# A PEER layer on one NeuronCore: the gate matrix from packed fp32 one-hots with one matmul per token, and the fetched token block picked first

## The chip, the cores and the metric

The kernel runs on one core of a Trainium2 chip. The metric is device time in microseconds for one execution. TensorE does the matmuls, VectorE (DVE), ScalarE (ACT) and GpSimd (POOL) do the element work, and SyncE (SP) starts most of the DMAs. Each engine works through its own queue of instructions in order.

## What is computed

A diffusion layer: a token mixer (two bidirectional scans), then PEER, a product-key retrieval over 128 x 128 experts for 512 latent tokens of width 1024. The change lies in PEER:

```python
PEER_HEADS = 8; PEER_NKEYS = 128; PEER_TOPK = 16; PEER_BLOCK = 128
def block(t):                                   # 128 tokens
    q = (t @ w_query).reshape(PEER_BLOCK, PEER_HEADS, 2, PEER_DQ // 2)
    s1 = jnp.einsum('thd,nd->thn', q[:, :, 0], k1)
    s2 = jnp.einsum('thd,nd->thn', q[:, :, 1], k2)
    v1, i1 = lax.top_k(s1, PEER_TOPK)
    v2, i2 = lax.top_k(s2, PEER_TOPK)
    cand_s = (v1[..., :, None] + v2[..., None, :]).reshape(PEER_BLOCK, PEER_HEADS, PEER_TOPK * PEER_TOPK)
    cand_i = (i1[..., :, None] * PEER_NKEYS + i2[..., None, :]).reshape(...)
    top_s, pos = lax.top_k(cand_s, PEER_TOPK)
    idx = jnp.take_along_axis(cand_i, pos, axis=-1)
    g = jax.nn.softmax(top_s, axis=-1)
    act = jax.nn.gelu(jnp.einsum('thkd,td->thk', expert_u[idx], t))
    return jnp.einsum('thk,thkd->td', g * act, expert_v[idx])
```

So every token picks 8 x 16 = 128 experts, each by a pair of key numbers (k1, k2) with a weight g.

## The kernel before

Token blocks 0 to 2 (384 tokens) are computed densely: every expert is evaluated for them, 128 experts (one first key) at a time, and a gate matrix, zero for experts that a token did not pick, weights the results. Block 3's 128 tokens are computed sparsely: the picked rows are fetched by index. Behind the mixer, PEER has four stages.

*Top stage* (from about 611 us). For each of 8 heads TensorE makes queries (pq, three fp32r matmuls for one product) and scores (pss, L727, plain fp32). VectorE's `pick_head` (L893) then finds a head's best 16 of each key list and of their sums. Before the change this loop picks blocks 0 to 2; block 3's scores are set aside in S3.

*Gate stage* (from 746.66 us, first L976, to 1155.89 us, last L990). `picks` (L920) turns places into key numbers, `gate_matrix` (L950) builds, for each token, the 128 x 128 matrix G[k2, k1] = sum over the 128 picks of onehot(k2) x g onehot(k1). For that, g is split into three bf16 parts. For 8 tokens at a time VectorE writes bf16 one-hots of both keys (`oh`, L976) and multiplies the first key's by the parts (`ohg`, L980 and L983; some by ScalarE, L979); TensorE does three bf16 matmuls per token (pG, L988), ScalarE copies four tokens' result to `stage` (L989), and a DMA writes 32 tokens to DRAM (Gd, L990). Block 3's pick_heads, its picks and the list of rows to fetch (`ix`) come after block 2, in the same stage.

The *hidden* part (L1004) of a group of 128 experts belongs to no stage alone: a row block ur of the first expert matrix is loaded, split into high (uh, ScalarE) and low parts (ul, GpSimd, L1001), 24 matmuls pH (L159 to L161) follow, and a gelu writes `gel`. AHEAD = 32 of 128 hiddens are written ahead of the main part, in a ring of AHEAD + 1 gel buffers; two PSUM buffers let TensorE run further ahead.

*Main part* (L1157 on). For each group: the next hidden, rows of the second matrix (vr, split to vh and vl), the gate weights of the group read back (G, L1020, one read per four groups), gel times G (`gated`, L1014, L1023), and 18 matmuls y (`combine`). Between them 264 `fetch_jobs` (L1042) are dealt evenly: an indirect DMA on GpSimd's queue (erow, L1052, six buffers), a dot product on VectorE (L1057), for the second matrix a weighted add (L1069). A *tail* finishes.

A tile framework's scheduler orders TensorE, VectorE, ScalarE and SyncE by its own costs; GpSimd's queue follows the program's order while fetches are under way (`manual_schedule`).

Of the kernel before, what the change touches and what calls it, by code (L numbers as in the profile page):

```python
# [15 lines left out]
OP = mybir.AluOpType  # L16
# [24 lines left out]
class Net:  # L41
# [3 lines left out]
    # ---------------------------------------------------------------- constants  # L45
# [16 lines left out]
    def scan_consts(self, c, tmp):  # L62
# [20 lines left out]
        # forget-gate lower bounds, channel on partition: [128, direction, head]  # L83
# [19 lines left out]
        # per-head norm gains along the row, gate weights  # L103
# [22 lines left out]
    def norm_stats(self, pool, x, tag):  # L126
        """mean and 1/std of the rows of x [128, 1024]"""
# [15 lines left out]
    def affine(self, out, x, stats, scale, shift, shared=None):  # L143
        """(x - mean) / std * scale + shift, on VectorE or, with a pool for the scratch, on ScalarE and GpSimd"""
# [50 lines left out]
    def mods_second(self, pers, pool):  # L195
        """g1, shift2, scale2, g2 of the latent stream: rows of w_ada^T times silu(c), one column each"""
# [26 lines left out]
    def mod_row(self, pool, ps, i, name, ptag):  # L223
        """vector i of m2 as a row on every partition"""
# [40 lines left out]
    # -------------------------------------------------------- input projection  # L265
# [967 lines left out]
```

## Time and profile before

| | us |
|---|---|
| time, median of 3 runs (2144.97, 2152.53, 2152.64) | 2152.53 |
| span of the profiled execution | 2142.0 |
| time of the profiled execution, taken as the median | 2152.5 |
| TensorE busy | 2016.0 (94%) |
| VectorE busy | 1578.8 (74%) |
| ScalarE busy | 808.4 (38%) |
| GpSimd busy | 1019.9 (48%) |
| TensorE's granted clock, mean | 0.904 |

The span runs from the first to the last instruction; the 10.5 us between it and the time are what lies around it. A busy TensorE is one that has a matmul under way; whether it is at its full speed tells the granted clock (1.00 is 2.4 GHz, the lower level is 1.2 GHz). A stretch is bound by the engine that never idles in it, or by the one that the others wait for. In the tables of stretches each engine's busy microseconds stand beside the length, and the counts of instructions in brackets.

### The profile page before, as it was taken

The page shows a single profiled execution, that of the slowest core. Times are in us where ns is not written, and L with a number is a line of the kernel's source. Part 1 is how long each engine was busy: PE and PEld are TensorE (multiplying, and loading weights), DVE is VectorE, ACT ScalarE, POOL GpSimd, SP SyncE. Part 2 cuts the span into 40 slices and gives each one's busy share as a digit, 9 for nine tenths or more (in the row PEclk, how much of TensorE's full clock was granted, in tenths as well). Part 3 has the DMA queues.
Part 4 walks back from the last instruction along what each step waited for, and adds up shares of the span by engine and source line. Part 5 has one row for each costly group of instructions (what it writes and reads, how often), then busy time and mean ns, then how long its engine had stood idle before and what let it go on. Part 6 is the DMA issues. An engine that isn't in the chain of part 4 may idle for free.

```text
span 2142.0 us, 27264 instructions
## 1 busy us (share of the span) xinstructions
PE 2016.0 (94%) x9973; PEld 1692.4 (79%) x9973; DVE 1578.8 (74%) x2640; ACT 808.4 (38%) x1253; POOL 1019.9 (48%) x637
## 2 busy tenths in 40 slices
PE   7877898897999899999999999999999999999997
PEld 2766777776778767777778889999889898998886
DVE  7799764767899953444437789899888889888546
ACT  3444443444343333433344333333333333333431
POOL 2445544545553310101102477777777777787001
PEclk9988999997999966667667999999999999999998
DMA  7544111001332121221214799898998989898343
GB/s 262 173 140 136 45 40 37 33 6 55 111 128 79 48 74 71 95 107 69 108 59 161 244 330 351 298 363 307 333 331 319 332 309 345 314 337 312 128 147 140
DMA packets 153031, 389.74 MB, mean 182 GB/s; under 512 B 12672, under 2 KB 62656, under 8 KB 151360
## 3 DMA queue, kind: packets, MB, share of 16 engines
q1 hardware_dynamic: 115456, 251.66, 33.6%
q0 software_dynamic: 36864, 134.23, 17.4%
q8 instruction: 78, 1.28, 0.2%
q10 hardware_dynamic: 576, 2.10, 0.2%
q14 instruction: 57, 0.47, 0.1%
HBM read 358.59 MB, written 29.36 MB: 181 GB/s over the span
## 4 chain that ended last, share of the span: by engine, by line
PE 63%; DVE 7%; issue 4%; DMA 4%; POOL 2%; ACT 1%; POOLq 0%; SPq 0%; DVEq 0%; ACTq 0%
PE pG L988 12%; PE pH L161 7%; PE pH L159 7%; PE pH L160 7%; PE y L160 7%; PE y L161 7%; PE y L159 6%; DMA erow<-in_v_dram,ix 2%; PE pq L160 1%; PE pq L161 1%; PE pq L159 1%; DMA ur<-in_uT_dram 1%; PE psc L512 1%; POOL ul L1001 1%; PE pss L727 1%
## 5 line engine op out<-in xcount | busy, mean ns | idle before, releaser
L1001 POOL TENSOR_TENSOR ul<-ur,uh 128x1024 fp32r<-128x1024 f32 x128 | 343.8, 2686 | 538.3 <-ACT uh L999 510.2
L161 PE MATMUL pH<-hh,ul 128*128 128x384 f32 x1024 | 371.5, 363 | 4.3 <-POOL ul L1001 4.2
L159 PE MATMUL pH<-hh,uh 128*128 128x384 f32 x1024 | 370.8, 362 | 2.4 <-ACT gel L1011 2.4
L160 PE MATMUL pH<-hl,uh 128*128 128x384 f32 x1024 | 369.6, 361 | 0.0
L160 PE MATMUL y<-vl,ah 128*128 128x512 f32 x768 | 302.6, 395 | 8.1 <-DVE vl L1001 4.0
L161 PE MATMUL y<-vh,al 128*128 128x512 f32 x768 | 301.4, 393 | 0.0
L159 PE MATMUL y<-vh,ah 128*128 128x512 f32 x768 | 299.3, 391 | 1.0 <-ACT vh L999 1.0
L988 PE MATMUL pG<-ohg,oh 128*128 128x128 bf16 x1152 | 273.5, 409 | 4.6 <-DVE ohg L980 4.0
L988 PEld LDWEIGHTS <-oh 128*128 128x128 bf16 x1152 | 166.0, 148 | 102.0 <-issue 15.2
L1069 DVE SCALAR_TENSOR_TENSOR yg<-erow,act,yg 128x1024 f32<-128x1024 f32 x127 | 195.4, 1539 | 54.4 <-DMA erow<-in_v_dram,ix 52.2
L999 ACT ACTIVATE uh<-ur 128x1024 fp32r<-128x1024 f32 x128 | 135.6, 1059 | 220.3 <-PE pH L160 117.1
L159 PEld LDWEIGHTS pH<-hh,uh 128*128 128x128 f32 x1024 | 211.1, 206 | 7.8 <-ACT gel L1011 2.7
L161 PEld LDWEIGHTS pH<-hh,ul 128*128 128x128 f32 x1024 | 210.7, 206 | 6.8 <-POOL ul L1001 5.2
L160 PEld LDWEIGHTS pH<-hl,uh 128*128 128x128 f32 x1024 | 210.5, 206 | 4.9
L976 DVE TENSOR_TENSOR oh<-iotaw,kT 128x2048 bf16<-128x2048 bf16 x48 | 59.1, 1232 | 208.0 <-PE pG L988 187.5
L1057 DVE SCALAR_TENSOR_TENSOR scr<-erow,h 128x1024 bf16<-128x1024 f32 x128 | 171.9, 1343 | 32.9 <-DMA erow<-in_u_dram,ix 31.5
L1052 POOL DMA_INDIRECT erow<-in_u_dram,ix x128 | 173.7, 1357 | 32.3 <-issue 23.9
L1052 POOL DMA_INDIRECT erow<-in_v_dram,ix x128 | 168.6, 1317 | 32.7 <-issue 20.2
L160 PEld LDWEIGHTS y<-vl,ah 128*128 128x128 f32 x768 | 144.8, 188 | 41.1 <-DVE vl L1001 7.3
L1001 DVE TENSOR_TENSOR vl<-vr,vh 128x1024 fp32r<-128x1024 f32 x127 | 165.5, 1305 | 12.9 <-ACT vh L999 12.9
L999 ACT ACTIVATE vh<-vr 128x1024 fp32r<-128x1024 f32 x128 | 134.6, 1054 | 93.6 <-DMA vr<-in_v_dram 68.0
L161 PEld LDWEIGHTS y<-vh,al 128*128 128x128 f32 x768 | 144.9, 189 | 29.9
(371 smaller groups left out, 3798.6 us busy)
## 6 DMA issues: line engine op xcount, KB each, us to landing
ur<-in_uT_dram SPq DMA_DIRECT2D x128, 512.0 KB
vr<-in_v_dram SPq DMA_DIRECT2D x128, 512.0 KB
Gd<-stage SPq DMA_DIRECT2D x12, 2048.0 KB
G<-Gd SPq DMA_DIRECT2D x32, 768.0 KB
wada<-in_w_ada_dram SPq DMA_DIRECT2D x64, 256.0 KB
wraw<-in_w_cf_dram SPq DMA_DIRECT2D x24, 512.0 KB
wada<-in_w_ada_dram SPq DMA_DIRECT2D x16, 512.0 KB
wqr<-in_w_q_dram SPq DMA_DIRECT2D x14, 512.0 KB
```

What stands on the lines that cost most here:

```text
L159: mm(out, lh, rh, start=start, stop=False)
L160: mm(out, lh, rl, start=False, stop=False)
L161: mm(out, ll, rh, start=False, stop=stop)
L512: nc.tensor.matmul(p[:, c, :], E[hp[h], 1, sl], E[hp[h], 0, sl], start=True, stop=True)
L727: nc.tensor.matmul(p[:, b, :], qT[s][:, b * 128:(b + 1) * 128], self.sk[:, s, :], start=True, stop=True)
L976: nc.vector.tensor_tensor(o, self.iota16w[:, :, None].to_broadcast([128, 128, 2, B]), wide(kT[:, None, :, t0:t0 + B]), op=OP.is_equal)
L988: nc.tensor.matmul(p[:, t, :], o[:, :, 1, t4 + t], f[:, :, j, t4 + t], start=j == 0, stop=j == 2)
L999: nc.scalar.activation(hi, raw, AF.Copy)
L1001: eng.tensor_tensor(lo, raw, hi, op=OP.subtract)
L1052: nc.gpsimd.indirect_dma_start(out=e, out_offset=None, in_=a[src], in_offset=bass.IndirectOffsetOnAxis(ap=self.ix[:, j:j + 1], axis=0))
L1057: nc.vector.scalar_tensor_tensor(scr, row("u", j), 1.0, h2, op0=OP.mult, op1=OP.mult, accum_out=dots[:, j:j + 1])
L1069: nc.vector.scalar_tensor_tensor(y, row("v", j), act[:, j:j + 1], y, op0=OP.mult, op1=OP.add)
```

## The change

The gate matrix. The key numbers and g of a block are transposed onto partitions as fp32 (`kg`), with no split. Per token VectorE makes two 128 x 128 fp32 operations on the row 0, 1, 2, ...: is_equal with k2, and is_equal with k1 times g; TensorE does one fp32 matmul, and ScalarE copies four tokens as before. The one-hots have three buffers of four tokens. The write of Gd per 32 tokens stays.

The order. The top loop picks all four blocks; block 3's picks, softmax and `ix` follow at once, ahead of the gate matrix. The fetch buffers open there, and `tick` deals the 264 fetch jobs over gate matrix (0.22 units per group of four tokens, one per hidden) and main part (one per hidden, one per group). In program order 43 jobs come to lie in the gate stage. GpSimd's program order begins ahead of the gate matrix. AHEAD goes from 32 to 25, and the hiddens are written between groups of tokens, not behind each block.

```diff
-    AHEAD = 32
-    GC, OB = 2, 2
+    AHEAD = 25
+    GB, OB = 4, 3
...
-    def gate_matrix(self, w, ps, b, key, g):
+    def picks_on_partitions(self, w, ps, key, g):
         p = ps.tile([128, 4, 128], F32, name="pkT", tag="ss", bufs=2)
         for i, t in enumerate((key[:, 0], key[:, 1], g)):
-            nc.tensor.transpose(p[:, i, :], t.rearrange("p h k -> p (h k)"), self.n.ident)
...
-        for q in range(128 // self.GT):
-            stage = w.tile([128, 128, self.GT], F32, name="stage", bufs=2)
-            for t8 in range(0, self.GT, B):
...
-                nc.vector.tensor_tensor(o, self.iota16w[:, :, None].to_broadcast([128, 128, 2, B]), wide(kT[:, None, :, t0:t0 + B]), op=OP.is_equal)
...
-                        for j in range(3):
-                            nc.tensor.matmul(p[:, t, :], o[:, :, 1, t4 + t], f[:, :, j, t4 + t], start=j == 0, stop=j == 2)
...
+            self.nc.tensor.transpose(p[:, i, :], t.rearrange("p h k -> p (h k)"), self.n.ident)
+        kg = w.tile([128, 3, 128], F32, name="kg", bufs=2)
+        self.nc.scalar.activation(kg, p[:, 0:3, :], AF.Copy)
+        return kg
+    def gate_group(self, w, ps, kg, t0, out, i):
+        nc, iota = self.nc, self.n.iota_row
+        GB = self.GB
+        o = w.tile([128, GB, 2, 128], F32, name="oh12", bufs=self.OB)
+        p = ps.tile([128, GB, 128], F32, name="pG", tag=("bd", "qp")[i % 2], bufs=2)
+        for t in range(GB):
+            k1, k2, g = (kg[:, j, t0 + t:t0 + t + 1] for j in range(3))
+            nc.vector.tensor_scalar(o[:, t, 0], iota, k2, None, op0=OP.is_equal)
+            nc.vector.tensor_scalar(o[:, t, 1], iota, k1, g, op0=OP.is_equal, op1=OP.mult)
+            nc.tensor.matmul(p[:, t, :], o[:, t, 0], o[:, t, 1], start=True, stop=True)
+        nc.scalar.activation(out, p.rearrange("p t n -> p n t"), AF.Copy)
...
-                        for b in range(ND):
+                        for b in range(4):
                             self.pick_head(w, S[:, b], b, h)
+                key = self.picks(w, 3)
+                self.softmax(w, self.g[:, None])
...
+                manual.enter_context(tc.manual_schedule(engines={mybir.EngineType.Pool}))
+                jobs = self.fetch_jobs(fp, fp, yg)
+                groups = ND * 128 // self.GB
+                gcost = 0.055 * self.GB
+                total = groups * gcost + 128 + 128 - self.TAIL - 24
+                done, spent = 0, 0.0
+                def tick(u):
+                    nonlocal done, spent
+                    spent += u
+                    want = min(len(jobs), int(len(jobs) * max(0, spent - 6) / (total - 6)))
+                    for f, *args in jobs[done:want]:
+                        f(*args)
+                    done = want
...
-                        self.gate_matrix(bp, ps, b, key, g)
-                        for _ in range(self.AHEAD // ND):
-                            self.hidden(nh, up, gl, hps)
-                            nh += 1
...
+                        for _ in self.gate_block(bp, ps, b, kg):
+                            at += 1
+                            tick(gcost)
+                            while nh < self.AHEAD * at // groups:
+                                self.hidden(nh, up, gl, hps)
+                                nh += 1
+                                tick(1)
```

What stands in the engines' queues. The names end in buffer numbers; lines of the changed kernel differ: its one-hots are L967 and L968, its pG L969, its ul L992, its fetch L1043, dots L1048, adds L1058 and L1060.

VectorE in the gate stage, before (`oh12` and `ohg` for eight tokens; `oh` rows belong to the next block's picks):

```order
L980 TENSOR_TENSOR ohg_6218<-oh12_6217,gp3_6172 128x128x16
L983 TENSOR_TENSOR ohg_6218<-oh12_6217,gp3_6172 128x128x6
L976 TENSOR_TENSOR oh12_6252<-iotaw_5039,kT_6170 128x2048
L945 TENSOR_TENSOR oh_7094<-oh_7094 128x8x64
L980 TENSOR_TENSOR ohg_6253<-oh12_6252,gp3_6172 128x128x16
L983 TENSOR_TENSOR ohg_6253<-oh12_6252,gp3_6172 128x128x6
L976 TENSOR_TENSOR oh12_6287<-iotaw_5039,kT_6170 128x2048
L945 TENSOR_TENSOR oh_7094<-oh_7094 128x8x32
L980 TENSOR_TENSOR ohg_6288<-oh12_6287,gp3_6172 128x128x16
```

VectorE where block 0 ends and block 1 begins, after (`pr`, `oh`, `key`: picks; `yg`: the fetched block's sums):

```order
L945 TENSOR_TENSOR oh_7167<-oh_7167 128x8x128
L1054 TENSOR_TENSOR act_6319<-act_6319,gp_4551 128x16
L928 TENSOR_SCALAR pr_7982<-pos2_5036 128x128
L945 TENSOR_TENSOR oh_7167<-oh_7167 128x8x64
L1058 TENSOR_SCALAR yg_4901<-erow_7563,act_6319 128x1024
L945 TENSOR_TENSOR oh_7167<-oh_7167 128x8x32
L1060 SCALAR_TENSOR_TENSOR yg_4901<-erow_7646,act_6319,yg_4901 128x1024
L946 TENSOR_TENSOR key_7159<-oh_7167 128x128
L1060 SCALAR_TENSOR_TENSOR yg_4901<-erow_7664,act_6319,yg_4901 128x1024
L967 TENSOR_SCALAR oh12_7181<-iota_row_59,kg_7178 128x128
L968 TENSOR_SCALAR oh12_7181<-iota_row_59,kg_7178 128x128
```

Three wide operations per eight tokens became two small ones per token, and additions of fetched rows, the last three of a run that begins with the tenth dot, now stand ahead of block 1's first one-hot.

GpSimd where the fetches begin, before, in the main part:

```order
L1001 TENSOR_TENSOR ul_9574<-ur_9571,uh_9573 128x1024
L1001 TENSOR_TENSOR ul_9636<-ur_9633,uh_9635 128x1024
L1052 DMA erow_9695<-in_u_dram,ix_4552 128x1024
L1052 DMA erow_9698<-in_u_dram,ix_4552 128x1024
L1001 TENSOR_TENSOR ul_9704<-ur_9701,uh_9703 128x1024
L1052 DMA erow_9763<-in_u_dram,ix_4552 128x1024
L1052 DMA erow_9766<-in_u_dram,ix_4552 128x1024
L1052 DMA erow_9769<-in_u_dram,ix_4552 128x1024
```

GpSimd within the gate stage, after (erow_7480 is the sixteenth fetch, the first for which all six buffers wait for dots that stand behind block 0's one-hots):

```order
L1043 DMA erow_7462<-in_u_dram,ix_4552 128x1024
L1043 DMA erow_7480<-in_u_dram,ix_4552 128x1024
L992 TENSOR_TENSOR ul_7531<-ur_7528,uh_7530 128x1024
L1043 DMA erow_7563<-in_v_dram,ix_4552 128x1024
L992 TENSOR_TENSOR ul_7616<-ur_7613,uh_7615 128x1024
L1043 DMA erow_7646<-in_v_dram,ix_4552 128x1024
L1043 DMA erow_7664<-in_v_dram,ix_4552 128x1024
L992 TENSOR_TENSOR ul_7715<-ur_7712,uh_7714 128x1024
L1043 DMA erow_7745<-in_v_dram,ix_4552 128x1024
L1043 DMA erow_7763<-in_v_dram,ix_4552 128x1024
```

The fetches moved from the main part to the gate stage, pairwise between the ul rows that the hiddens there need.

TensorE at the end of the gate stage, before (26 of 32 hiddens are done there):

```order
L988 LDWEIGHTS oh12_8597
L988 MATMUL pG_8618<-ohg_8598,oh12_8597 128x128
L160 MATMUL pH_8804<-hl_4550,uh_8800 128x384
L161 MATMUL pH_8804<-hh_4549,ul_8801 128x384
L159 MATMUL pH_8837<-hh_4549,uh_8833 128x384
L160 MATMUL pH_8837<-hl_4550,uh_8833 128x384
```

TensorE at the end of the gate stage, after (14 pH rows follow the last pG, then the first y of the main part):

```order
L161 MATMUL pH_9015<-hh_4549,ul_9012 128x384
L969 MATMUL pG_8802<-oh12_8801 128x128
L159 MATMUL pH_9015<-hh_4549,uh_9011 128x384
L969 MATMUL pG_8802<-oh12_8801 128x128
L160 MATMUL pH_9015<-hl_4550,uh_9011 128x384
L161 MATMUL pH_9015<-hh_4549,ul_9012 128x384
L159 MATMUL pH_9015<-hh_4549,uh_9011 128x384
```

Loads of bf16 weights and three matmuls per token became one fp32 matmul per token among pH rows; in the stage there are 384 pG and 469 pH in place of 1152 and 446, with 189 pH ahead of it in place of 176, and 27 of the hiddens done at its end, where before more were left to come.

## Rows read from the trace of the kernel before

**Rows 1.** The page: the chain that ended last, by engine and line
```profile
PE pG L988 12%; PE pH L161 7%; PE pH L159 7%; PE pH L160 7%; PE y L160 7%; PE y L161 7%; PE y L159 6%; DMA erow<-in_v_dram,ix 2%; PE pq L160 1%; PE pq L161 1%; PE pq L159 1%; DMA ur<-in_uT_dram 1%; PE psc L512 1%; POOL ul L1001 1%; PE pss L727 1%
```

**Rows 2.** Stretches: start:end, length, busy us of each engine, granted clock, DMA share, GB/s
```profile
640.00:660.00 20.00, 20.00 (x104) 16.65 (x103) 18.39 (x129) 7.34 (x14) 8.34 (x4) 1.00 0.24 80
900.00:950.00 50.00, 50.00 (x200) 38.24 (x199) 21.21 (x24) 20.22 (x30) 7.65 (x3) 0.67 0.20 74
1150.00:1200.00 50.00, 45.83 (x238) 42.62 (x237) 43.74 (x117) 20.35 (x28) 25.75 (x8) 0.91 0.62 214
1300.00:1350.00 50.00, 50.00 (x255) 45.49 (x254) 48.15 (x45) 18.22 (x25) 38.79 (x25) 1.00 0.95 346
```

**Rows 3.** Timeline (start, us, engine, line), VectorE and SyncE: the gate stage's ends
```profile
746.66 1.56 DVE L976 TENSOR_TENSOR oh<-iotaw,kT 128x2048 bf16<-128x2048 bf16 x1
...
1155.89 0.33 SPq L990 DMA_DIRECT2D Gd<-stage  x1
```

**Rows 4.** The page's groups: busy, mean ns, then idle time before and its releaser
```profile
L988 PE MATMUL pG<-ohg,oh 128*128 128x128 bf16 x1152 | 273.5, 409 | 4.6 <-DVE ohg L980 4.0
...
L976 DVE TENSOR_TENSOR oh<-iotaw,kT 128x2048 bf16<-128x2048 bf16 x48 | 59.1, 1232 | 208.0 <-PE pG L988 187.5
```

**Rows 5.** Timeline of TensorE, 879 to 891 us
```profile
879.68 0.52 PE L160 MATMUL pH<-hl,uh 128*128 128x384 f32 x1
880.00 0.52 PE L161 MATMUL pH<-hh,ul 128*128 128x384 f32 x1
...
881.28 5.71 PE L988 MATMUL pG<-ohg,oh 128*128 128x128 bf16 x24
...
890.51 0.33 PE L159 MATMUL pH<-hh,uh 128*128 128x384 f32 x1
890.69 0.33 PE L160 MATMUL pH<-hl,uh 128*128 128x384 f32 x1
```

**Rows 6.** Timeline of TensorE: scores of the last head
```profile
709.16 2.06 PE L727 MATMUL pss<-sk,qT 128*128 128x128 f32 x16
710.99 0.42 PE L159 MATMUL pH<-hh,uh 128*128 128x384 f32 x1
```

**Rows 7.** Timeline of VectorE and GpSimd: small rows alone, and under a ul
```profile
8.57 0.28 DVE L56 TENSOR_SCALAR ident<-iota_row,lane 128x128 f32<-128x128 f32 x1
8.76 0.28 DVE L69 TENSOR_TENSOR xo<-si,ti 128x128 int32<-128x128 int32 x1
...
720.58 2.39 POOL L1001 TENSOR_TENSOR ul<-ur,uh 128x1024 fp32r<-128x1024 f32 x1 [1.78 <-ACT uh L999]
...
721.00 2.07 DVE L928 TENSOR_SCALAR pr<-pos 128x128 uint32<-128x128 uint32 x1
...
723.84 0.20 DVE L928 TENSOR_SCALAR pr<-pos 128x128 uint32<-128x128 uint32 x1
723.96 0.08 DVE L876 MATCH_VALUE_LOAD i<-v,resta 128x8 f32 x1
```

**Rows 8.** Groups by line and shape (busy, mean ns): 128x128 with an immediate
```profile
L76 DVE TENSOR_SCALAR mlo<-xf 128x128 f32<-128x128 f32 x7 | 1.6, 227 | 0.2
```

**Rows 9.** Timeline of GpSimd and VectorE: first fetch and first dot
```profile
1228.06 1.28 POOL L1052 DMA_INDIRECT erow<-in_u_dram,ix  x1 [0.18 <-issue]
...
1238.58 1.22 DVE L1057 SCALAR_TENSOR_TENSOR scr<-erow,h 128x1024 bf16<-128x1024 f32 x1
```

**Rows 10.** Stretches, the line of ul on GpSimd alone
```profile
746.00:1156.00 410.00, 54.52 (x21) 0.67 0.22 84
```

**Rows 11.** Stretches, VectorE alone: one head of the top stage, the whole
```profile
657.70:670.56 12.86, 12.05 (x85) 1.00 0.28 90
611.21:746.66 135.45, 126.82 (x708) 0.95 0.26 86
```

**Rows 12.** One line's instructions (ns min/median/max, first and last start): gated row
```profile
L1023 DVE TENSOR_TENSOR gel<-gel,G x128: 543/552/2789, 1176.8 to 1991.9; 128x384 f32<-128x384 f32 x128
```

**Rows 13.** Stretches: an early one with gaps on TensorE
```profile
100.00:120.00 20.00, 11.85 (x61) 11.12 (x62) 20.00 (x27) 7.37 (x14) 11.97 (x7) 0.57 0.36 119
```

More of the change, by code (lines that the diff above doesn't have):

```diff
@@ L683, in out_proj @@
                 self.yg = pers.tile([128, D], F32, name="yg")
-                self.S0 = self.yg[:, 0:768].rearrange("p (b s n) -> p b s n", b=3, s=2)
+                self.S0 = self.yg.rearrange("p (b s n) -> p b s n", b=4, s=2)
                 self.scores(self.q0, ps, "pht", [((0, 2), lambda s: self.S0[:, 0:2, s, :])])
@@ L993, in load_split, with gate_block @@
+    def gate_block(self, w, ps, b, kg):
+        nc, GT, GB = self.nc, self.GT, self.GB
+        for q in range(128 // GT):
+            stage = w.tile([128, 128, GT], F32, name="stage", bufs=2)
+            for i in range(GT // GB):
+                self.gate_group(w, ps, kg, q * GT + i * GB, stage[:, :, i * GB:(i + 1) * GB], i)
+                if i == GT // GB - 1:
+                    nc.sync.dma_start(self.Gd[b * (128 // GT) + q], stage)
+                yield
     def load_split(self, rpool, pool, src, tag, bufs=2, far=True, rbufs=2):
@@ L1114, in run @@
             up = up_es.enter_context(tc.tile_pool(name="uring", bufs=1, side="right", reuse_waits="tile"))
+            fp = up_es.enter_context(tc.tile_pool(name="fetch", bufs=1, side="right", reuse_waits="tile"))
             nh = 0
+            manual = up_es.enter_context(ExitStack())
             with ExitStack() as e1:
@@ L1124, in run @@
                 nc.gpsimd.tensor_copy(self.iota16, n.iota_row[:, 0:16, None].to_broadcast([128, 16, 16]))
-                self.iota16w = w.tile([128, 128, 8], BF, name="iotaw")
-                nc.gpsimd.tensor_copy(self.iota16w, n.iota_row[:, :, None].to_broadcast([128, 128, 8]))
-                S3 = w.tile([128, 8, 2, 128], F32, name="S3")
                 with tc.tile_pool(name="wq", bufs=1, reuse_waits="tile") as wp:
@@ L1142, in run @@
                             self.softmax(w, tsd)
-                        key, g = self.picks(w, b), tsd[:, b]
-                        self.gate_matrix(bp, ps, b, key, g)
-                        for _ in range(self.AHEAD // ND):
-                            self.hidden(nh, up, gl, hps)
-                            nh += 1
-                    for h in range(8):
-                        self.pick_head(w, S3[:, h], 3, h)
-                    key = self.picks(w, 3)
-                    self.softmax(w, self.g[:, None])
-                    nc.vector.scalar_tensor_tensor(self.ix, key[:, 0].rearrange("p h k -> p (h k)"), 128.0,
-                                                   key[:, 1].rearrange("p h k -> p (h k)"), op0=OP.mult, op1=OP.add)
-                    while nh < self.AHEAD:
-                        self.hidden(nh, up, gl, hps)
-                        nh += 1
+                        key = self.picks(w, b)
+                        kg = self.picks_on_partitions(bp, ps, key, tsd[:, b])
+                        for _ in self.gate_block(bp, ps, b, kg):
[5 more added lines that the diff above has]
+                                tick(1)
             with ExitStack() as e1:
@@ L1160, in run @@
                 self.y = [tuple(yp.tile([128, 512], F32, name=f"y{b}{hf}") for hf in range(2)) for b in range(ND)]
-                with tc.tile_pool(name="fetch", bufs=1, reuse_waits="tile") as fp, \
-                        tc.manual_schedule(engines={mybir.EngineType.Pool}):
-                    jobs = self.fetch_jobs(fp, fp, yg)
-                    done, spent, total = 0, 0, 2 * (128 - self.AHEAD) + self.AHEAD - self.TAIL - 24
-                    for i in range(128 - self.TAIL):
-                        spent += 1
-                        if nh < 128:
-                            self.hidden(nh, up, gl, hps)
-                            nh += 1
-                            spent += 1
-                        v = self.rows(i, w, w, 2)
-                        ops = self.gated(i, w, w, 2), v
-                        for b in range(ND):
-                            self.combine(i, b, ops)
-                        want = min(len(jobs), len(jobs) * max(0, spent - 12) // (total - 12))
-                        for f, *args in jobs[done:want]:
-                            f(*args)
-                        done = want
+                for i in range(128 - self.TAIL):
+                    if nh < 128:
+                        self.hidden(nh, up, gl, hps)
+                        nh += 1
+                        tick(1)
+                    v = self.rows(i, w, w, 2)
+                    ops = self.gated(i, w, w, 2), v
+                    for b in range(ND):
+                        self.combine(i, b, ops)
+                    tick(1)
+                tick(total)
                 up_es.close()
```

39 lines of the change are left out of this document (6 added, 33 removed).

## The prediction

> **What bounds the kernel now.** I read the chain of work that ended last, then the stretches, then who waits for whom. In the chain the largest line is L988, the gate matrix's matmuls, at 12% of the span [rows 1]; it all lies in one stage. In the table of stretches [rows 2] that is the one at 900 us: TensorE busy for 50.00 of 50 us, at a granted clock of 0.67, VectorE for 21; ahead of it (640) and behind it (1300) the clock is 1.00. The gate stage lasts from the first one-hot at 746.66 to the last block's write at 1155.89 [rows 3], 409 us. TensorE bounds it, and VectorE waits: 187.5 us of its idle time ahead of the one-hots end on a pG [rows 4]. The main part is TensorE's too (50.00 of 50 us at 1300), with the DMA queues at 0.95.
>
> Inside the gate stage, 24 pG take 5.71 us less their tail, 0.217 us each; around them two pH follow each other by 0.32 us, and some microseconds later by 0.18 [rows 5]. 0.32 against 0.174 to 0.18 is the lower of the two levels (1.2 GHz) against the upper. 1152 pG [rows 4] x 0.217 = 250 us: that, and hidden-layer matmuls that also partly run at the low level, make the 409.
>
> **Part 1: the gate matrix.** Removed: 1152 pG, 48 each of three wide VectorE operations, 96 of ScalarE. Added: per token one fp32 matmul and two VectorE operations of 128x128 fp32, 384 and 768 in all.
>
> TensorE: the nearest row of an fp32 matmul with 128 columns is the scores' pss. Sixteen records (two to a matmul) start at 709.16, and the next matmul starts at 710.99 [rows 6]: 1.83/8 = 0.229 us each at the upper level, so 0.45 at the lower. 384 of them are 88 us (173 at the lower level) in place of 250. With them run 469 pH by the new order of instructions, 0.174 each, 82 us (0.32 each, 150). TensorE needs 170 us of the stage at the upper level, 323 at the lower.
>
> VectorE: an is_equal of 128x128 fp32 against one per-partition value stands in the trace once: 0.28 us long, the next starts 0.19 later [rows 7]. With an immediate the same shape takes 0.227 [rows 8], so a per-partition value costs 0.05; the second operation has two of them: 0.335 long, the next 0.255 later, an estimate. A token costs 0.19 + 0.255 = 0.445 us, 384 tokens 171 us. The bounds: the closest spacing of any 128x128 row with a scalar, 0.12 from 723.84 to 723.96 [rows 7], gives some 100 us for 768; the whole durations, 0.28 + 0.335, give 236. I take 171, since the row it comes from is the same operation.
>
> Besides, VectorE does in the stage 32 operations of the fetch at 1.22 us (the first dot, [rows 9]; the adds taken alike), 39 us, and the picks of blocks 1 and 2, 20. And it loses time to GpSimd: a 0.20 us row takes 2.07 at 721.00, under the GpSimd ul of 720.58 [rows 7], 1.8 us a piece; the stage of before holds 21 ul [rows 10], and I count 20, 36 us. Sum: 171 + 39 + 20 + 36 = 266 us. So VectorE becomes the bound of the stage, if TensorE's mean clock stays above 170/266 = 0.64.
>
> A page of the Trainium skill speaks against this step: "VectorE: DVE Perf Modes", section "The TRN2 errata — SBUF-src ops pay a fixed extra latency per instruction", says that each small operand pays a fixed cost and advises tiles of 512 elements or more. By its cycle formula, 58 + 128 at 0.96 GHz, an operation would be 0.194 us, an estimate, 768 of them 149 us, and the forecast below 22 us lower; its note that the measured fixed part is nearer 150 cycles comes out at 0.22 us for 64 further cycles, which the 0.227 of [rows 8] bears out.
>
> **Part 2: the fetched block first.** In the top stage one head of three blocks costs VectorE 12.05 of the 12.87 us that TensorE gives it, 4.0 us a pick head [rows 11]. Eight more pick heads are 32 us, of which 6 fall into slack. To them come picks and softmax of block 3, 10 (from the 126.8 us of the whole top stage, less 24 x 4.0: 30 for a softmax, one block's picks, part of another's), and nine dots that the order puts ahead of the first one-hot, 11. About 9 us of block 1's picks, which stood ahead of it, fall behind. 26 + 10 + 11 - 9 = 38: the first one-hot goes from 746.7 to about 785. TensorE does not wait uselessly all that time; 189 pH in place of 176 stand ahead of its first pG.
>
> **Part 3: the fetches in the gate stage.** GpSimd issues in program order, six erow buffers. VectorE's order holds dot 10 behind all 256 one-hot operations of block 0; the sixteenth fetch needs its buffer, so it and the ul behind it on GpSimd's queue wait there. Then VectorE in turn has dots 10 to 16 and three adds ahead of block 1's first one-hot. From issue to first dot is 10.5 us [rows 9]; fetch 16 and three more with two ul between them (1.3 and 2.4 us each) make about 22, of which dots and picks cover 16 to 18. 6 us of wait at each of two borders: 12. Bounds: 3 (all covered) and 25 each (nothing covered). Filling and draining the stage: 5, worked out as one group of four tokens with its copy on either side.
>
> Gate stage: 266 + 12 + 5 = 283, so it ends at 785 + 283 = 1068 where it ended at 1156.
>
> **Part 4: what comes behind.** From 1156 to the end were 986 us. 36 more pH (469 + 189 less 446 + 176) are done ahead of it: -6. Before, TensorE filled the time from the last pG to the first gated row with hiddens: Gd write 1155.89 [rows 3], first gated row 1176.8 [rows 12], which makes some 24 us with the splits behind it up to the first y; it idled about 4 of the 50 us from 1150 on, by the table of stretches [rows 2]. Now the ring holds 25 hiddens and is full with 14 pH rows left (2.4 us) when the last pG is done: 22 us idle, +22 - 4, and 3 for the clock, which falls meanwhile. The main part's fetches become sparser (221 jobs in 199 units in place of 264 in 188): -3, since TensorE waits there only for a few microseconds; bounds 0 and -10. 986 - 6 + 18 + 3 - 3 = 998.
>
> The span is 1068 + 998 = 2066. The profiled execution has a span of 2142.0 and about 10.5 us around it by the median of 2152.5, so I forecast **2077 us**, 3.5% less. The three runs lie between 2145.0 and 2152.6.
>
> **Rivals.**
>
> *VectorE is quicker than priced.* At 100 us for the one-hots VectorE needs 195 and TensorE, 170 us at a mean clock of 0.75, needs 227: the stage ends near 785 + 227 + 12 = 1024, the time is 2033, and with half of the boundary's idle time covered 2020. For it: small rows do overlap [rows 7]. Against: the one is_equal there doesn't run that closely.
>
> *The clock stays low.* TensorE now waits for one-hots token by token. Early in the kernel, in 100 to 120 us, it was busy for 11.85 of 20 us, and the clock was 0.57 [rows 13]. With 323 us of low-level work TensorE is the bound again: 785 + 323 + 12 + 5 = 1125, time 2134; the two-pointer operation at its whole duration (236 + 95 + 17 = 348) would give 2142 with nearly the same end. Against: a TensorE that is the bound has no gaps, and the stages where it had none show 1.00 at 640 and 1300 [rows 2], though the old pG without gaps did not. The Trainium skill, "TensorE: Matmul & The Clock Gate", section "HAM oscillation — how this bites in real kernels", tells of kernels whose recurring waits drop the clock, so that each burst begins low; by that rule this rival holds (here [rows 5] show low-level pH right behind the pG and upper-level pH further on).
>
> *Slower: low clock and borders add up.* If TensorE runs at the low level and the borders are uncovered at 25 us each (ul behind a blocked fetch, VectorE behind that fetch's landing, TensorE out of hiddens), the stage is 323 + 50 + 5 = 378, and with a boundary of 25 us rather than 22 and 3 us more at the low level behind it the time is 785 + 378 + 998 + 6 + 10.5 = 2178. It decides from a stage of 370 us on. For it: GpSimd's in-order queue. Against: the two don't go together well, since long waits of VectorE leave TensorE time to catch up.
>
> *The spread fetch does not spread.* That half is already in the forecast: 32 of 264 jobs fall in the stage, in three clumps. If they cost nothing, 39 + 12 us less, near 2026.
>
> **How the numbers follow.** Forecast (2050 to 2100): 0.52. Quicker, by the first or the last rival (2016 to 2050): 0.17. Low clock or full durations (2100 to 2145, a quarter of it above 2142): 0.2. The slower one (above 2163): 0.08; 0.03 lies between. A measurement of this kernel can tell about 0.5% from no change, 2142 to 2163. Faster 0.52 + 0.17 + 0.15 = 0.84, same 0.05 + 0.03 = 0.08, slower 0.08. The range from 2020 to 2140 leaves out 0.02 below and 0.16 above.
>
> **What would show it.** In the profile of the changed kernel: VectorE busy nearly throughout the gate stage, and TensorE's idle time there released by the one-hots; one-hot rows 0.28 and 0.33 long; the first one-hot near 785 and the last pG near 1068; the stage's clock above 0.64; two stalls of some 6 us where GpSimd waits for a dot; after the last pG an idle TensorE of some 20 us that ends on the G read. Wrong would be: a TensorE that is busy throughout the stage at the low level, or waits of VectorE for erow of more than 25 us.

## The result, and the profile after

The changed kernel takes 2074.67 us (median of four runs, 2071.08 to 2076.52). Against the kernel before the ratio is 0.9652, 95% interval 0.9635 to 0.967: 3.5% faster. The forecast was 2077 us.

The profiled execution took 2075.31 us with a span of 2073.5. The chain of work that ended last, by line, from the page of the profile:

```profile
PE y L160 8%; PE y L161 8%; PE y L159 8%; PE pH L161 6%; PE pH L159 6%; PE pH L160 6%; DVE oh L968 4%; DVE oh L967 3%; DMA erow<-in_u_dram,ix 1%; PE psc L512 1%; DVE cand L902 1%; DVE scr L1048 1%; DVE oh L945 1%; DVE i L876 1%; DVE resta L874 1%
```

pG, the first entry in [rows 1], is gone from the list; VectorE's two one-hot lines stand in its place, with 7% of the span instead of 12. The stages, as in [rows 2] (start:end, length, then busy us of TensorE, its weight loads, VectorE, ScalarE and GpSimd, the granted clock, the DMA share, GB/s): the gate stage, the time from its last pG to the first y, and the rest.

```profile
800.60:1083.80 283.20, 227.21 (x1253) 199.28 (x1252) 274.63 (x863) 85.13 (x138) 100.08 (x56) 0.88 0.51 188
1083.80:1106.40 22.60, 2.17 (x13) 1.85 (x11) 17.35 (x19) 3.24 (x6) 11.91 (x8) 0.62 0.97 355
1106.40:2073.50 967.10, 950.20 (x4720) 853.09 (x4720) 685.84 (x733) 335.97 (x470) 564.97 (x304) 1.00 0.76 262
```

In the gate stage VectorE is busy for 274.63 of 283.20 us; it waited for TensorE before, now TensorE (227.21) is the one that waits. The granted clock there is 0.88, where [rows 2] had 0.67. Behind the stage TensorE does next to nothing for 22 us; then it is the bound again.

The one-hots, in VectorE's timeline (start, us) and in groups over the stage (busy, mean ns, then idle time before them):

```profile
802.89 0.27 DVE L967 TENSOR_SCALAR oh<-iota_row,kg 128x128 f32<-128x128 f32 x1
803.09 0.33 DVE L968 TENSOR_SCALAR oh<-iota_row,kg 128x128 f32<-128x128 f32 x1
803.35 0.27 DVE L967 TENSOR_SCALAR oh<-iota_row,kg 128x128 f32<-128x128 f32 x1
```

```profile
L968 DVE TENSOR_SCALAR oh<-iota_row,kg 128x128 f32<-128x128 f32 x384 | 135.6, 353 | 0.0
L967 DVE TENSOR_SCALAR oh<-iota_row,kg 128x128 f32<-128x128 f32 x384 | 119.2, 310 | 8.7 <-PE pG L969 8.2 <-ACT kg L956 0.3
L1048 DVE SCALAR_TENSOR_TENSOR scr<-erow,h 128x1024 bf16<-128x1024 f32 x19 | 28.1, 1478 | 0.1
L1060 DVE SCALAR_TENSOR_TENSOR yg<-erow,act,yg 128x1024 f32<-128x1024 f32 x15 | 23.3, 1555 | 0.0
```

A token takes 0.46 us, 802.89 to 803.35. The means, 353 and 310 ns, lie above the 333 and 273 ns of undisturbed rows (the medians of the two lines): 255 us of busy time where 384 x 0.606 make 232. Rows overlap a little, so busy times of groups add up to more than the time they cover.

### The profile page after: what moved, and what is told of

It reads as the page before. It is cut to its first block, busy times and chain, and to the rows that moved or that the text cites. A ratio compares the mean times of both kernels' runs of the same rounds, so it can differ in the third digit from the quotient of the medians.

```text
span 2073.5 us, 27025 instructions
## 1 busy us (share of the span) xinstructions
PE 1835.7 (89%) x9589; PEld 1588.4 (77%) x9589; DVE 1612.0 (78%) x3246; ACT 731.6 (35%) x1141; POOL 1042.4 (50%) x636
## 4 chain that ended last, share of the span: by engine, by line
PE 47%; DVE 19%; issue 8%; DMA 3%; POOL 2%; ACT 1%; POOLq 0%; SPq 0%; DVEq 0%; ACTq 0%
PE y L160 8%; PE y L161 8%; PE y L159 8%; PE pH L161 6%; PE pH L159 6%; PE pH L160 6%; DVE oh L968 4%; DVE oh L967 3%; DMA erow<-in_u_dram,ix 1%; PE psc L512 1%; DVE cand L902 1%; DVE scr L1048 1%; DVE oh L945 1%; DVE i L876 1%; DVE resta L874 1%
## 5 line engine op out<-in xcount | busy, mean ns | idle before, releaser
L992 POOL TENSOR_TENSOR ul<-ur,uh 128x1024 fp32r<-128x1024 f32 x128 | 344.7, 2693 | 288.5 <-ACT uh L990 288.0
L161 PE MATMUL pH<-hh,ul 128*128 128x384 f32 x1024 | 360.0, 352 | 44.4 <-POOL ul L992 44.4
L159 PE MATMUL pH<-hh,uh 128*128 128x384 f32 x1024 | 359.8, 351 | 34.2 <-ACT gel L1002 32.8
L159 PE MATMUL y<-vh,ah 128*128 128x512 f32 x768 | 299.3, 391 | 20.4 <-ACT ah L1017 20.4
L1060 DVE SCALAR_TENSOR_TENSOR yg<-erow,act,yg 128x1024 f32<-128x1024 f32 x127 | 197.6, 1556 | 116.3 <-DMA erow<-in_v_dram,ix 115.7
L1048 DVE SCALAR_TENSOR_TENSOR scr<-erow,h 128x1024 bf16<-128x1024 f32 x128 | 194.5, 1519 | 101.0 <-DMA erow<-in_u_dram,ix 100.5
L1043 POOL DMA_INDIRECT erow<-in_u_dram,ix x128 | 184.7, 1443 | 174.8 <-DVE scr L1048 107.7
L161 PEld LDWEIGHTS pH<-hh,ul 128*128 128x128 f32 x1024 | 199.0, 194 | 47.0 <-POOL ul L992 46.9
L159 PEld LDWEIGHTS pH<-hh,uh 128*128 128x128 f32 x1024 | 199.3, 195 | 39.9 <-ACT gel L1002 34.6
L1043 POOL DMA_INDIRECT erow<-in_v_dram,ix x128 | 180.4, 1409 | 79.7 <-DVE yg L1060 44.3
L992 DVE TENSOR_TENSOR vl<-vr,vh 128x1024 fp32r<-128x1024 f32 x127 | 198.6, 1565 | 10.8 <-ACT vh L990 10.8
L159 PEld LDWEIGHTS y<-vh,ah 128*128 128x128 f32 x768 | 144.6, 188 | 48.6 <-ACT ah L1017 20.8
L969 PE MATMUL pG<-oh 128*128 128x128 f32 x768 | 162.2, 306 | 15.4 <-DVE oh L968 13.6
L1017 ACT ACTIVATE ah<-gel 128x384 fp32r<-128x384 f32 x128 | 66.5, 524 | 285.5 <-PE y L160 249.9
L969 PEld LDWEIGHTS pG<-oh 128*128 128x128 f32 x768 | 131.9, 199 | 38.9 <-DVE oh L968 21.7
```

What stands on the lines that cost most here:

```text
L159: mm(out, lh, rh, start=start, stop=False)
L161: mm(out, ll, rh, start=False, stop=stop)
L969: nc.tensor.matmul(p[:, t, :], o[:, t, 0], o[:, t, 1], start=True, stop=True)
L992: eng.tensor_tensor(lo, raw, hi, op=OP.subtract)
L1017: nc.scalar.activation(ah, g, AF.Copy)
L1043: nc.gpsimd.indirect_dma_start(out=e, out_offset=None, in_=a[src], in_offset=bass.IndirectOffsetOnAxis(ap=self.ix[:, j:j + 1], axis=0))
```

## The experiments

All ran on the chip beside the kernel before; times are medians, ratios are to it. A table of the profiled executions first (us from the span's start); the stage is first one-hot to last pG, the gap last pG to first y, the rest from there to the end. The time is the median of all executions; the profiled one can lie some us off it (the first experiment's was its fastest, 7 us below the median).

| kernel | first one-hot | stage | gap | rest | span | time | ratio, interval |
|---|---|---|---|---|---|---|---|
| before | 746.7 | 408 | 36 | 951 | 2142.0 | 2151.1 | |
| changed | 800.6 | 282.6 | 23.2 | 967.1 | 2073.5 | 2074.7 | 0.9652 (0.9635 to 0.967) |
| 1 gate matrix alone | 744.3 | 252.9 | 26.1 | 965.3 | 1988.6 | 1997.4 | 0.9293 (0.9259 to 0.9326) |
| 2 fetches in main part | 790.5 | 238.3 | 14.9 | 971.6 | 2015.3 | 2024.6 | 0.9414 (0.9384 to 0.9444) |
| 3 ul on VectorE | 798.0 | 256.8 | 26.4 | 973.4 | 2054.6 | 2054.6 | 0.9546 (0.9508 to 0.9585) |
| 4 half of k2 | 803.1 | 240.7 | 25.1 | 965.0 | 2033.9 | 2038.1 | 0.9469 (0.9431 to 0.9507) |
| 5 gate alone, ul on VectorE | 739.5 | 226.7 | 26.8 | 969.1 | 1962.1 | 1962.5 | 0.9119 (0.9088 to 0.915) |
| 6 the same, AHEAD = 36 | 746.6 | 234.4 | 33.9 | 952.6 | 1967.5 | 1968.7 | 0.9145 (0.9102 to 0.9187) |
| 7 early pick, no spread | 787.0 | 249.2 | 17.4 | 954.5 | 2008.1 | 2012.4 | 0.9362 (0.934 to 0.9383) |
| 8 changed, AHEAD = 18 | 795.1 | 257.7 | 22.6 | 996.7 | 2072.1 | 2079.7 | 0.9677 (0.9644 to 0.971) |
| 9 as 5, wide k2 | 744.4 | 213.3 | 31.1 | 959.2 | 1948.0 | 1948.7 | 0.9043 (0.8996 to 0.9089) |

(The gap of before is full of hiddens, 32 of 36 us; the first experiment's holds 16 us of them, the changed kernel's 2. Two executions of one kernel, the fifth, differ by 4.4 us in the first one-hot and by 5.7 in the rest, so differences of that size between single spans say little.)

### 1. The gate matrix alone

The kernel before with `picks_on_partitions`, `gate_group` and `gate_block` in place of `gate_matrix`; nothing else moves but the hiddens.

```diff
-                        self.gate_matrix(bp, ps, b, key, g)
-                        for _ in range(self.AHEAD // ND):
-                            self.hidden(nh, up, gl, hps)
-                            nh += 1
+                        kg = self.picks_on_partitions(bp, ps, key, g)
+                        for _ in self.gate_block(bp, ps, b, kg):
+                            at += 1
+                            while nh < self.AHEAD * at // (ND * 128 // self.GB):
+                                self.hidden(nh, up, gl, hps)
+                                nh += 1
```

> The kernel before with the new gate matrix alone: block 3 is picked behind the gate matrix and fetched in the main part as before, AHEAD = 32, hiddens dealt between the groups of tokens. Theory A (VectorE bounds the gate stage, and fetch operations put there lengthen it one for one, while in the main part they are hidden under TensorE): first one-hot at 747, stage 175 (one-hots) + 22 (picks) + 40 (lost to GpSimd) = 237 us, last pG near 985, then block 3's selection, some 45 us of VectorE, with TensorE idle for 25 us of it; 986 us behind it; span about 1975, time 1977 (1960 to 2000). Theory B (the early pick and the spread of the fetches carry the gain): the main part, as dense as before, and the late selection give back most of it, time above 2050.

Measured: 1997.4 us, 77 us less than the changed kernel. Theory A had 1977, B over 2050. The stage was 253 us rather than 237, since some 8 us of block 3's selection came to lie in it, and its one-hots and picks lose more to GpSimd than estimated:

```profile
L968 DVE TENSOR_SCALAR oh<-iota_row,kg 128x128 f32<-128x128 f32 x384 | 155.6, 405 | 0.0
L967 DVE TENSOR_SCALAR oh<-iota_row,kg 128x128 f32<-128x128 f32 x384 | 123.2, 321 | 1.3 <-ACT kg L956 1.3
```

That is 279 us of busy time against 232 undisturbed, with 27 operations of GpSimd, its ul, in the stage (the last busy time of the row):

```profile
744.30:997.50 253.20, 213.28 (x1385) 201.18 (x1384) 253.20 (x836) 92.33 (x149) 64.57 (x27) 0.97 0.39 146
```
What follows: the new gate matrix, with the hiddens dealt between its groups of tokens (the two were not tested apart), is worth 154 us of time; the other half of the change costs half of that again.

### 2. The fetches back in the main part

```diff
-                total = groups * gcost + 128 + 128 - self.TAIL - 24
+                total = 2 * (128 - self.AHEAD) + self.AHEAD - self.TAIL - 24
-                    want = min(len(jobs), int(len(jobs) * max(0, spent - 6) / (total - 6)))
+                    want = min(len(jobs), int(len(jobs) * max(0, spent - 12) / (total - 12)))
-                            tick(gcost)
-                                tick(1)
```

> The changed kernel with all 264 fetch jobs in the main part, at the density of the kernel before (block 3 is still picked first, AHEAD stays 25). Theory A: the nine dots ahead of the first one-hot and the 34 fetch operations within the stage go, 11 + 42 + 5 us of VectorE and its collisions; first one-hot near 775, last pG near 1010, the idle time of TensorE behind it stays at 20 us; time about 2010 (1995 to 2030). Theory B (the spread is worth something because the main part is relieved): not faster than 2060.

Measured: 2024.6 us, within what theory A gave; B falls. The times differ by 50 us, the spans of the profiled executions by 58.2, and the table says where: first one-hot 10.1 earlier (790.5, not near the 775 that theory A had), stage 44.3 shorter, gap 8.3 shorter, rest 4.5 longer. So the spread costs 63 us ahead of the main part, and what it relieves there, 4.5 us, is no more than the scatter. The gap had been part of neither theory: expected were 20 us again. The first gate read goes out 7.3 us behind the last gate write (SyncE's timeline of this run), and the first y follows at 1043.7:

```profile
1029.74 0.32 SPq L980 DMA_DIRECT2D Gd<-stage  x1
1030.25 0.33 SPq L987 DMA_DIRECT2D vr<-in_v_dram  x1
1037.03 0.38 SPq L1011 DMA_DIRECT2D G<-Gd  x1
```

In the changed kernel the same pair lies 9.5 us apart:

```profile
1084.18 0.33 SPq L980 DMA_DIRECT2D Gd<-stage  x1
1087.04 0.33 SPq L987 DMA_DIRECT2D ur<-in_uT_dram  x1
1087.55 1.24 SPq L987 DMA_DIRECT2D vr<-in_v_dram  x1
1093.67 0.38 SPq L1011 DMA_DIRECT2D G<-Gd  x1
```

and its first y comes 12.7 us behind the read where here it takes 6.7, with the DMA share at 0.97 in its gap and 0.84 in this run's. That the fetches on the same DMA engines slow the write and the read fits these numbers; it is not shown.

### 3. The ul of the gate stage on VectorE

```diff
-                                self.hidden(nh, up, gl, hps)
+                                self.hidden(nh, up, gl, hps, False)
```

(`far` goes through to `load_split`, so the subtraction runs on VectorE.)

> The changed kernel with the 25 ul of the gate stage on VectorE instead of GpSimd (1.22 us each there, as vl has it). If a ul on GpSimd costs VectorE about 2 us by collision, the stage gets shorter by 0.8 us x 19 = 15 us and GpSimd's queue holds no ul back: time 2050 to 2062. If the collisions cost less than 1.2 us each, or the hiddens now wait in VectorE's queue, time 2075 to 2090.

Measured: 2054.6 us, 20 less. 16 ul lie within the stage, where the changed kernel has 19 on GpSimd. The groups of that stage:

```profile
L968 DVE TENSOR_SCALAR oh<-iota_row,kg 128x128 f32<-128x128 f32 x384 | 131.3, 342 | 0.0
L967 DVE TENSOR_SCALAR oh<-iota_row,kg 128x128 f32<-128x128 f32 x384 | 110.0, 287 | 3.2 <-ACT kg L956 3.1
L1048 DVE SCALAR_TENSOR_TENSOR scr<-erow,h 128x1024 bf16<-128x1024 f32 x18 | 21.9, 1216 | 0.0
L992 DVE TENSOR_TENSOR ul<-ur,uh 128x1024 fp32r<-128x1024 f32 x16 | 19.4, 1213 | 0.0
```

The one-hots fall from 254.8 to 241.3 us, the dots from 1478 to 1216 ns each. VectorE does 19.4 us more work and is done earlier: work taken from GpSimd and given to the engine that bounds the stage pays off. Its waits fell too, from 8.7 to 3.2 us, so this run alone does not tell the collisions from a freer queue of GpSimd; the fifth experiment, with no fetches in the stage, does.

### 4. Half of the k2 one-hots left out

```diff
-            nc.vector.tensor_scalar(o[:, t, 0], iota, k2, None, op0=OP.is_equal)
-            nc.tensor.matmul(p[:, t, :], o[:, t, 0], o[:, t, 1], start=True, stop=True)
+            if t % 2 == 0:
+                nc.vector.tensor_scalar(o[:, t, 0], iota, k2, None, op0=OP.is_equal)
+            nc.tensor.matmul(p[:, t, :], o[:, t - t % 2, 0], o[:, t, 1], start=True, stop=True)
```

> The changed kernel with the one-hot of k2 left out for every second token (the matmul takes its neighbour's). If VectorE bounds the stage: 192 x 0.195 = 37 us less, time 2038 (2030 to 2046). If TensorE at the lower clock level bounds it: no change, 2070 to 2077.

Measured: 2038.1 us, 36.5 less, for 37 expected. VectorE's operations stand on the path one for one; TensorE, with the same matmuls, does not bound the stage.

### 5, 6. Gate matrix alone, with ul on VectorE, and more hiddens ahead

Both edits of the first and the third experiment, and in the sixth one line more.

```diff
-                                self.hidden(nh, up, gl, hps)
+                                self.hidden(nh, up, gl, hps, False)
...
-    AHEAD = 32
+    AHEAD = 36
```

> The kernel before with the new gate matrix alone (as the first experiment), with the ul of the hiddens in the gate stage on VectorE. If a GpSimd ul costs VectorE more than doing it there, as the third experiment had it (20 us for 25 ul): time 1977 (1968 to 1986). If that gain came from GpSimd's queue, which held ul behind fetches there and holds no fetches here: 1997, no change.

Measured: 1962.5 us, 35 less than the first experiment and more than the 20 expected. A second measurement beside the ninth experiment gave 1960.2 (ratio 0.912, 0.9064 to 0.9176; expected as follows).

> The fifth experiment's kernel once more, beside the wide one on the same chip: 1962 (1955 to 1970).

The one-hots now run nearly undisturbed, in groups of 740 to 1010 us:

```profile
L968 DVE TENSOR_SCALAR oh<-iota_row,kg 128x128 f32<-128x128 f32 x384 | 128.5, 335 | 0.0
L967 DVE TENSOR_SCALAR oh<-iota_row,kg 128x128 f32<-128x128 f32 x383 | 105.1, 275 | 0.0
L992 DVE TENSOR_TENSOR ul<-ur,uh 128x1024 fp32r<-128x1024 f32 x26 | 31.5, 1211 | 0.0
```

They took 278.8 us in the first experiment, 233.6 here: the 27 ul on GpSimd had cost the one-hots 45 us, 1.7 each, and cost VectorE 1.21 each when it does them. That makes 14 of the 26 us by which the stage got shorter; the other 12 are picks and selection, which ran into ul as well and held somewhat more of block 3 there. The stage:

```profile
739.50:966.50 227.00, 222.37 (x1391) 202.47 (x1390) 227.00 (x856) 91.75 (x150) 1.55 (x1) 1.00 0.43 163
```

Both engines are full, at a granted clock of 1.00.

> The same with AHEAD = 36. If TensorE has idle time left in the gate stage, each hidden moved there saves 4.2 us of the main part and costs VectorE 1.2: 4 x 3 = 12 us less than the run with 32, time 1965 (1957 to 1974). If TensorE is full there, no less than with 32.

Measured: 1968.7 us, not faster than with 32; the intervals overlap. By the line above TensorE had only 5 us of idle time left, and what leaves the main part (rest 952.6 instead of 969.1) comes back in stage and gap, 14.8 us, and in a first one-hot 7.1 us later.

### 7. Early pick without the spread

As the second, with the fetch buffers opened in the main part.

```diff
-    AHEAD = 25
+    AHEAD = 32
-            fp = up_es.enter_context(tc.tile_pool(name="fetch", bufs=1, side="right", reuse_waits="tile"))
...
+                fp = e1f.enter_context(tc.tile_pool(name="fetch", bufs=1, reuse_waits="tile"))
+                manual.enter_context(tc.manual_schedule(engines={mybir.EngineType.Pool}))
+                jobs += self.fetch_jobs(fp, fp, yg)
                 for i in range(128 - self.TAIL):
```

> The changed kernel with all fetches in the main part and, since the fetch buffers then open only there, AHEAD = 32 (the second experiment had 25). Seven hiddens more in the gate stage: 29 us less in the main part, 7 x 1.8 = 13 us more of VectorE's time in the stage, time 2009 (2000 to 2018): the early pick of block 3 costs the other 12 us against the first experiment. If the early pick is free, the 27 us between the first and the second experiment are AHEAD's alone: 1997.

Measured: 2012.4 us, inside the first range, outside the second. The early pick costs 15 us against the first experiment, 19.5 by the spans: the first one-hot comes 42.7 us later, and stage, gap and rest, where the selection no longer lies, give 23.2 back. With the second experiment this splits the 77 us that the other half of the change costs: 15 for the early pick, 12 for AHEAD at 25 rather than 32 (2024.6 less 2012.4), 50 for the spread (2074.7 less 2024.6).

### 8. Fewer hiddens ahead

```diff
-    AHEAD = 25
+    AHEAD = 18
```

> The changed kernel with AHEAD = 18 instead of 25. If hiddens in the gate stage run in idle time of TensorE and cost VectorE 1.8 us each: 7 x (4.2 - 1.8) = 17 us more, time 2091 (2085 to 2098). If TensorE bounds the stage, what leaves it comes back in the main part: 2075, no change.

Measured: 2079.7 us, below the first theory's range; the intervals of this kernel and the changed one overlap, so by the time alone the second theory stands. The stage decides between them (columns as above): it is VectorE's to the last 0.05 us, so the second theory's reason does not hold either:

```profile
795.10:1053.00 257.90, 213.74 (x1126) 177.91 (x1124) 257.85 (x845) 77.74 (x126) 81.07 (x42) 0.91 0.48 177
```

The rest grew by 29.6 us, as worked out, but the stage shrank by 24.9 and not by 13. The groups of that stretch say why the 1.8 us a hidden was too low a price:

```profile
L968 DVE TENSOR_SCALAR oh<-iota_row,kg 128x128 f32<-128x128 f32 x384 | 136.5, 355 | 0.0
L967 DVE TENSOR_SCALAR oh<-iota_row,kg 128x128 f32<-128x128 f32 x384 | 110.2, 287 | 0.2 <-ACT kg L956 0.2
L1060 DVE SCALAR_TENSOR_TENSOR yg<-erow,act,yg 128x1024 f32<-128x1024 f32 x15 | 19.3, 1284 | 0.0
L1048 DVE SCALAR_TENSOR_TENSOR scr<-erow,h 128x1024 bf16<-128x1024 f32 x13 | 15.8, 1212 | 0.0
```

13 dots in place of 19 (15.8 us, not 28.1), since `tick(1)` brings fetch jobs with each hidden; one-hots 246.7 us, not 254.8; adds 4 less; and 8 us of waiting gone. Against that, picks and the first sum of fetched rows took some 9 us more by their rows. A hidden in the stage cost what it saved behind it.

### 9. Four k2 one-hots in one operation

```diff
+        nc.vector.tensor_tensor(o[:, :, 0], iota[:, None].to_broadcast([128, GB, 128]),
+                                kg[:, 1, t0:t0 + GB, None].to_broadcast([128, GB, 128]), op=OP.is_equal)
-            nc.vector.tensor_scalar(o[:, t, 0], iota, k2, None, op0=OP.is_equal)
```

> The fifth experiment's kernel with the four k2 one-hots of a group as one 128x512 operation instead of four of 128x128. The traces have 128x512 fp32 operations of two tensors at 0.69 us with the next some 0.61 later, four small ones take 0.78: if VectorE still bounds the stage and a small operand's fixed part is what it pays, 96 x 0.17 = 16 us less, time 1947 (1940 to 1955). If reading both operands by broadcast runs slower than that, or TensorE bounds the stage by now, no change: 1958 to 1968.

Measured: 1948.7 us, 11.5 less than the same kernel without it on the same chip (1960.2), for 16 expected. The two intervals overlap, but each of the four executions (1944.5 to 1950.6) lies below each of the other kernel's (1954.0 to 1971.5). In groups over 735 to 960 us:

```profile
L969 DVE TENSOR_SCALAR oh<-iota_row,kg 128x128 f32<-128x128 f32 x384 | 105.8, 333 | 0.0
L965 DVE TENSOR_TENSOR oh<-iota_row,kg 128x512 f32<-128x512 f32 x96 | 64.9, 676 | 0.0
```

One wide operation took 0.676 us, 64.9 in all, where 384 small ones had 105.1. The stage shrank by 13.4 us:

```profile
744.40:957.70 213.30, 201.33 (x1388) 194.92 (x1387) 213.30 (x600) 92.27 (x149) 1.40 (x1) 1.00 0.45 171
```

TensorE (201.33 of 213.30 us busy) is by now close to the bound itself. This is the fastest kernel of the study, 126 us (6%) below the changed one.

## Why the prediction was right, point by point

**The bound changes hands.** Right. TensorE had bounded the stage at a granted clock of 0.67; VectorE bounds it now, and the half of k2 left out gave 36.5 us for 37. The clock was 0.88, above the 0.64 that the argument needed, so the rival with the low clock did not come about. TensorE's idle time in the stage is released by the one-hots, as forecast, and, twice as much of it, by ul that stood behind a fetch on GpSimd's queue, which the forecast did not name:

```profile
PE pH L161 <- POOL ul L992: 27.5, 4, 10.2
PEld pG L969 <- DVE oh L968: 21.7, 73, 2.8
PE pG L969 <- DVE oh L968: 13.6, 9, 2.6
DVE oh L967 <- PE pG L969: 8.2, 1, 8.2
```

(engine line waited for: us in total, times, longest, of 800.6 to 1084.)

**The stage's sum.** 283 us forecast, 283.2 measured to the last copy, and most terms came close. One-hots undisturbed, 0.45 to 0.46 from token to token, 175 for 384 (171 forecast, by an is_equal that stood in the trace of before once; [rows 7, 8]). Fetch operations: 35 at 1.22, 43 (39). Picks: 25 by the rows of experiment 3 (20). Collisions: 22 us on the one-hots, 9 on dots and adds, some 9 on the picks, by their means over those of undisturbed rows, 40 (36). Waiting 8.6 in place of 12 + 5. These make 292; some 8 us are ends of rows that overlap the next row and count twice. So four terms came out 4 to 5 us larger than forecast, and the waits and the overlap took that back: that the sum fits to the microsecond is luck.

**The borders.** Half right. GpSimd's queue stood for 51, 36 and 33 us behind a dot or an add, as the order had let expect, but between the blocks VectorE did not wait for the landings: dots, adds, picks and their collisions covered them. (The 22 us of the prediction are 19 by its own rows: 10.5 + 3 x 1.3 + 2 x 2.4.) It waited once, for 8.2 us, 24 tokens before the end of block 1, in another way than said: a fetch's issue took 10.17 us on GpSimd, the ul behind it came late, TensorE waited for it, and the one-hots for TensorE.

```profile
869.24 1.15 POOL L1043 DMA_INDIRECT erow<-in_u_dram,ix  x1 [51.08 <-DVE scr L1048]
...
938.06 10.17 POOL L1043 DMA_INDIRECT erow<-in_v_dram,ix  x1 [36.21 <-DVE yg L1060]
948.25 2.35 POOL L992 TENSOR_TENSOR ul<-ur,uh 128x1024 fp32r<-128x1024 f32 x1
```

```profile
950.65 0.69 PE L161 MATMUL pH<-hh,ul 128*128 128x384 f32 x1 [10.20 <-POOL ul L992]
```

**The start, mis-sized.** Forecast 785, measured 800.6. The eight pick heads are right: the last row of the last one starts 26.5 us later than before, for 26 (first before, then changed).

```profile
726.04 0.25 DVE L876 FIND_INDEX8 pos<-tsd,restb 128x8 uint32<-128x100 f32 x1
752.54 0.26 DVE L876 FIND_INDEX8 pos<-gp,restb 128x8 uint32<-128x100 f32 x1
```

From there to the first one-hot it was 20.6 us before and is 48.1 now: 27.4 more, where 10 + 11 - 9 = 12 had been put down. The nine dots, put at 11, took 12.9, and VectorE waited 5.6 for them, which the step had at nothing:

```profile
L1048 DVE SCALAR_TENSOR_TENSOR scr<-erow,h 128x1024 bf16<-128x1024 f32 x9 | 12.9, 1433 | 5.6 <-DMA erow<-in_u_dram,ix 5.5
```

The other 8 us lie in the 9 and the 10: of block 1's picks only some 3 us, not 9, had stood ahead of the first one-hot before, and block 3's picks and softmax took some 12. Taking the dots away (experiment 2) did not give their 18 us back, only 10: six small rows there ran into ul on GpSimd and lost some 12 us together. One of them, 0.28 us long when undisturbed, under the ul of 781.02:

```profile
782.77 2.47 DVE L933 SCALAR_TENSOR_TENSOR prf<-pf 128x128 bf16<-128x128 bf16 x1
```

**Behind the stage, mis-sized the other way.** Forecast 998, measured 989.3 from the last Gd write (1084.18) to the end. The idle boundary is there, 20.4 us for 22 (PE y L159 <- ACT ah L1017). Of the 3 us for the clock about half shows: the granted clock is 0.54 from the first y to 1110, where y start 0.43 us apart, and 1.00 from 1110 on, where they start 0.23 apart. The whole stretch, before and changed (columns as in [rows 2]):

```profile
1155.89:2142.00 986.11, 962.77 (x4768) 862.83 (x4767) 803.48 (x879) 347.04 (x481) 621.63 (x360) 0.99 0.82 291
1084.18:2073.50 989.32, 952.00 (x4731) 854.57 (x4729) 702.80 (x751) 338.86 (x474) 576.50 (x312) 0.99 0.76 264
```

TensorE idles 14 us more, where 18 had been put down, and is busy for 10.8 us less, where 6 had been put down for the 36 pH. Where the other 5 us of busy time went is open; the 3 us of the sparser fetches may be among them.

**The span and the time.** The 10.5 us between the profiled span and the median of before were no overhead: in all four runs of the changed kernel the time lies 1.8 us above the span. The profiled execution of before was one of its faster ones, and the median of others stood beside its span. So the span was forecast at 2066 and is 2073.5, and three errors (start +15.6, behind the stage -8.7, span to time -8.7) nearly cancel in 2077 for 2074.7. That the time fits to 2 us is luck; the mechanism and the stage are what was right.

**What the prediction did not ask.** It priced the fetches ahead of the main part at 11 + 39 + 12 us and still took the change as one thing; that -76 is -154 from the gate matrix and +77 from the rest. The spread's share of that, 50 us, could have been read from its own sum, in which every fetch operation moved there stands on VectorE's path, while [rows 2] had shown the main part full on TensorE whatever VectorE did. The rival "the spread fetch does not spread" even gave 2026 for a stage without fetches; the run without them came to 2024.6, closer than it had to, since the 2026 still hold the 11 us of the nine dots.

## What to carry to other kernels

When a stage's bound moves to another engine, work of that engine moved into the stage lands on the path; leave it where another engine bounds, even if that place looks crowded. A subtraction on GpSimd beside small operations of VectorE can cost VectorE more (1.7 us on the one-hots here) than doing it there (1.21 us). And split a change with several parts before judging it: here one part gained 154 us, and the other gave half of it back.

## What was not expected of the hardware

- An indirect fetch's issue on GpSimd, 0.93 to 2.01 us in every kernel whose fetches all lie in the main part, took 10.17 us at 938.06, while VectorE ran one-hots without a pause. It is not the only one: experiment 8 has one of 9.13 and one of 5.65, experiment 3 three of 4.42 to 5.81, all ahead of the main part and under rows of VectorE that follow each other without a gap. What holds the issue up was not tested. The longest of experiment 8:

```profile
941.30 9.13 POOL L1043 DMA_INDIRECT erow<-in_v_dram,ix  x1 [45.25 <-DVE yg L1060]
```

- fp32 matmuls with gaps between them ran at a granted clock of 0.88 to 1.00 in the gate stages here, while the stage of before with its bf16 ones, without gaps, had 0.67 [rows 2]. The Trainium skill, "TensorE: Matmul & The Clock Gate", section "HAM oscillation — how this bites in real kernels", tells of a kernel whose recurring waits for DMA drop the clock; the traces here show the stage with waits at the higher clock, so waits alone do not tell it. What held it down before is open.
- One 128x512 operation of two broadcast fp32 operands took 0.676 us and the next row started 0.60 after it, while four 128x128 ones with a scalar take 0.8 from start to start (0.20 each, 802.89 to 803.09). The Trainium skill's advice to prefer operands of 512 elements ("VectorE: DVE Perf Modes", "The TRN2 errata — SBUF-src ops pay a fixed extra latency per instruction") holds here: 11.5 us for 96 groups.
